# A hybrid encoder layer on one core: the conv branch's token order moves from the rounding and the remainder to the norm's product

## The chip, the cores and the metric

The kernel runs on one core of a Trainium2 chip. The metric is the device time of one execution in microseconds (us); the kernel before takes 1026.38 us, the median of three runs. The core has five engines that each work through a queue of their own in order and wait for one another by semaphores: TensorE (PE, matmuls, results in PSUM banks), VectorE (DVE), ScalarE (ACT), GpSimd (POOL) and SyncE (SP, which here only issues DMAs).

## The reference

One encoder layer over 1024 tokens of 1024 numbers. A convolution branch and an attention branch share the input projection and, side by side, the output projection. The branch that matters here:

```python
def conformer_conv(a, gate, dw_kernel, dw_bias, ln_g, ln_b):
    u = a * jax.nn.sigmoid(gate)
    y = lax.conv_general_dilated(u, dw_kernel[:, None, :], ...)   # depthwise, 31 taps over positions
    y = y + dw_bias
    y = layer_norm(y, ln_g, ln_b)      # over the 512 channels of a token
    return jax.nn.silu(y)
...
        mix = jnp.concatenate([conv_out, attn_out], axis=-1)
        x = x + mix @ w_out[l]
        h = rms_norm(x, norm2_g[l])
        x = x + (jax.nn.silu(h @ w_gate[l]) * (h @ w_up[l])) @ w_down[l]
```

## The kernel before

All matmuls work on numbers split in two: a rounded part in a shorter format (called hi, or the cast) and the remainder (lo). The helper `split` makes both: ACT rounds, and DVE or POOL subtracts the rounded part from the source (lines 108 and 112). The helper `mac` (lines 116 to 118) makes one product of three matmuls: hi by hi, hi by lo of the moving side, lo of the weights by hi.

The token axis is cut in two halves of 512, h = 0 and 1. The attention works on tokens in the order of blocks of the 2-D grid, and its output tiles `at` hold that order: within a half, 4 column blocks b, 16 columns j, 8 rows i. The convolution needs the tokens in their natural order (i, b, j), so its result has to change order before it meets `at` in the output projection. The conv result lies in tiles `u`, one for each of the 4 chunks c of 128 channels; the projection reads its split copies `cm[h]`.

The layer norm of the conv branch goes in steps for each half h: `conv_mean` (PE sums the channels, tile `mr`), `conv_dev` (DVE subtracts the mean at line 894, ACT squares at line 896 into tiles `sd`, POOL adds two of them and DVE the others at lines 898 to 900), `conv_var` (PE transposes into `vs`, DVE sums rows at line 906, ACT takes the root, DVE the reciprocal), `conv_rows` (PE spreads the reciprocals over all partitions, tile `vr` in PSUM, line 918), `conv_norm` for each chunk (DVE multiplies `u` by `vr`, line 921), and `conv_silu` for each chunk (ACT at line 925, then the split into `cm`). In the kernel before, `conv_norm` works in place and in natural order, and the split reads `u` with a step so that `cm` gets the other order.

The output projection `proj` fills banks `pj`, eight blocks m of 128 outputs by two halves: `acc[m, h]`, four k blocks from `at` (k = 4 to 7) and four from `cm` (k = 0 to 3). The kernel runs blocks m = 0 to 3 of half 0 and m = 0, 1 of half 1 over `at` first; each product calls `weave`, which runs the next entry of a list, `woven`. The steps above are placed in it by `slots`, numbered 0 to 19. Then follow the products of `cm` for half 0, k by k, four banks each, with the rest of the `conv_silu` calls woven in. When bank m is complete, `resid` (line 935) adds the input on DVE and frees the bank; block m = 4 needs the bank of m = 0.

The weights of the output projection come in chunks named `wo` + half of the outputs + first k (wo00, wo02, wo04, ...). `take` splits the next one. `WO_SUB` says which engines subtract its halves or quarters: an entry (pool, dve) gives the first half of the columns to POOL and the second to DVE; four times pool makes four pieces on POOL.

The order on every engine is the order in which the code emits instructions; no scheduler changes it.

Of the kernel before, what the change touches and what calls it, by code (L numbers as in the profile page):

```python
# [8 lines left out]
AF = mybir.ActivationFunctionType  # L9
OP = mybir.AluOpType  # L10
# [55 lines left out]
def body(tc, a):  # L66
    from contextlib import ExitStack
    with ExitStack() as ctx:
        build(ctx, tc, a)


def build(ctx, tc, a):
    nc = tc.nc
    pe, act, dve, pool = nc.tensor, nc.scalar, nc.vector, nc.gpsimd
# [5 lines left out]
    def T(tag, shape, bufs, name, dt=F32):  # L80
        return sb.tile(shape, dt, tag=tag, bufs=bufs, name=name)
# [10 lines left out]
    def ST(name, dt=F32):  # L92
        return T("st", [P, 512], 5, name, dt)

    def SM(name, n=8):
        return T("sm", [P, 8], 12, name)[:, :n]
# [4 lines left out]
    def tp(name):  # L101
        return ps.tile([P, 512], F32, tag="tp", bufs=2, name=name)
# [4 lines left out]
    def split(hi, lo, src, sub=(pool,)):  # L107
        act.copy(hi, src)  # L108
        n = src.shape[-1] // len(sub)
        for i, eng in enumerate(sub):  # L110
            sl = slice(i * n, (i + 1) * n)
            eng.tensor_tensor(*[w[..., sl] for w in (lo, src, hi.bitcast(F32))], OP.subtract)  # L112
# [25 lines left out]
    def want(src, name, dst, sub=(pool,)):  # L138
        chunks.append((src, name, dst, sub))
# [72 lines left out]
    def wo_dst(d, k0):  # L212
        def dst():
            if (d, k0 // 4) == (1, 1):
                if not woq:
                    woq.append(H(f"wo{d}{k0}", F32R))
                o = k0 % 4 * 1024
                hl = (woq[0][:, o:o + 1024], woq[0][:, o + 1024:o + 2048])
            else:
                hl = (G(f"wo{d}{k0}h", F32R), G(f"wo{d}{k0}l", F32R))  # L220
            for j in range(2):
                wo[d, k0 + j] = [w[:, j * 512:(j + 1) * 512] for w in hl]
            return hl
        return dst

    WO_SUB = {(0, 2): (pool,) * 4, (1, 0): (dve, pool), (1, 2): (dve, pool), (1, 4): (pool, dve), (1, 6): (pool, dve)}
    for d in range(2):
        for k0 in (4, 6, 0, 2):
            want(a["wo"][k0 * P:(k0 + 2) * P, d * 512:(d + 1) * 512].rearrange("(k p) m -> p k m", p=P),
                 f"wo{d}{k0}", wo_dst(d, k0), WO_SUB.get((d, k0), (pool,)))  # L230

# [34 lines left out]
    eps = T("eps", [P, 1], 1, "eps")  # L266
    dve.memset(eps, EPS)
    warm = SM("warm", 1)
# [410 lines left out]
    def whole(n):  # L679
        return -(-n // 32) * 32  # L680
# [36 lines left out]
    def groups(s_):  # L717
        n, m = width(s_), P if s_ == 0 else 4 * WIN[order[s_][1]][1]
        return [slice(o, min(o + m, n)) for o in range(0, n, m)]
# [66 lines left out]
    def weigh(i):  # L786
        s_, hp = divmod(i, 4)
        rh, cb = order[s_]
        if hp == 0:
            os_[s_] = tp(f"o{s_}").rearrange("p (c q) -> p c q", c=4)  # L790
        gs = groups(s_)
        for g, k in enumerate(gs):
            n = whole(k.stop - k.start)
            v = vwt["first"][:, g, :] if s_ == 0 else vw[cb, rh + g]
            for hh in range(2):
                c = (2 * hp + hh) * HD
                pe.matmul(os_[s_][hh * HD:(hh + 1) * HD, hp], v[:n, c:c + HD], pTs[i][hh][:n, g],  # L797
                          start=g == 0, stop=g == len(gs) - 1)

    def half(name):  # L800
        w = H(name, F32R).rearrange("p (w k s) -> p w k s", w=2, s=512)
        return w[:, 0], w[:, 1]

    def at_of(s_):
        rh, cb = order[s_]
        return [w[:, :, cb * P:cb * P + P] for w in at[rh]]

    def evac_hi(s_):
        if not at:
            at.extend(half(f"at{h}") for h in range(2))  # L810
        act.copy(at_of(s_)[0], os_[s_])

    def evac_lo(s_):
        hi, lo = at_of(s_)
        dve.tensor_tensor(lo, os_[s_], hi.bitcast(F32), OP.subtract)
# [48 lines left out]
    cm, xT, acc = [], {}, {}  # L864
# [15 lines left out]
    cw = {}  # L880

    def of(c, h):
        return u[c][0][:, h * 512:(h + 1) * 512]

    def conv_mean(h):
        cw["m", h] = tp(f"mr{h}")
        for n, w in enumerate(cr[:2]):
            pe.matmul(cw["m", h], cr[2], w[:, h * 512:(h + 1) * 512], start=n == 0, stop=n == 1)

    def conv_dev(h):  # L890
        sq = []
        for c in range(4):
            w = of(c, h)
            dve.scalar_tensor_tensor(w, cw["m", h], -1.0 / 512, w, OP.mult, OP.add)
            sq.append(ST(f"sd{h}{c}"))
            act.activation(sq[c], w, AF.Square)
            if c == 1:
                pool.tensor_tensor(sq[0], sq[0], sq[1], OP.add)
        dve.tensor_tensor(sq[2], sq[2], sq[3], OP.add)
        dve.tensor_tensor(sq[0], sq[0], sq[2], OP.add)  # L900
        cw["s", h] = sq[0]

    def column_rstd(r, pt, w, n):
        for t in range(4):
            pe.transpose(pt[:, t * P:(t + 1) * P], w[:, t * P:(t + 1) * P], ident)
        dve.tensor_reduce(r, pt.rearrange("p (t c) -> p t c", c=P), mybir.AxisListType.X, OP.add)
        act.activation(r, r, AF.Sqrt, bias=eps, scale=1.0 / n)
        dve.reciprocal(r, r)

    def conv_var(h):  # L910
        pt = tp(f"vs{h}")
        cw["v", h] = SM(f"cv{h}", 4)
        column_rstd(cw["v", h], pt, cw["s", h], DC)

    def conv_rows(h):
        cw["r", h] = tp(f"vr{h}")
        for t in range(4):
            pe.transpose(cw["r", h][:, t * P:(t + 1) * P], cw["v", h][:, t:t + 1].to_broadcast([P, P]), ident)

    def conv_norm(h, c):  # L920
        dve.tensor_tensor(of(c, h), of(c, h), cw["r", h], OP.mult)

    def conv_silu(h, c):
        w = of(c, h)
        act.activation(w, w, AF.Silu, bias=lnb[:, c:c + 1], scale=lng[:, c:c + 1])
        hi, lo = [q[:, c].rearrange("p (b j i) -> p b j i", b=4, j=16) for q in cm[h]]
        split(hi, lo, w.rearrange("p (i b j) -> p b j i", b=4, j=16), (dve,))

    def load_xT(m):
        xT[m] = G(f"xT{m}")  # L930
# [14 lines left out]
    for i in range(4, 32, 2):  # L945
# [31 lines left out]
        if jobs:  # L977
# [22 lines left out]
    conv_dev(0)  # L1000

    cm += [half(f"cm{h}") for h in range(2)]
    slots = {0: lambda: (weigh(31), evac_hi(7), evac_lo(7)), 3: lambda: (conv_var(0), conv_mean(1), conv_dev(1)),
             7: lambda: (conv_rows(0), [conv_norm(0, c) for c in range(4)]), 13: lambda: conv_var(1),
             16: lambda: conv_rows(1), 17: lambda: act.activation(warm, eps, AF.Silu),
             19: lambda: (conv_silu(0, 0), conv_norm(1, 0))}
    woven.extend(slots.get(n, lambda: None) for n in range(20))
    ATTN, CONV = (4, 5, 6, 7), (0, 1, 2, 3)
    take()
# [12 lines left out]
    for m in range(4):  # L1022
        load_xT(m)
    later = [(0, c) for c in range(1, 4)] + [(1, c) for c in range(4)]
    woven.extend(lambda q=q: (conv_norm(1, q[1]) if q[0] == 0 else None, conv_silu(*q)) for q in later)
    for k in CONV:
        for m in range(4):
# [491 lines left out]
    def quarter(w, o, t):  # L1519
        return w[:, o + t * 512:o + t * 512 + 512]  # L1520
# [58 lines left out]
    for half in range(2):  # L1579
        acc, part_ = GB[half][:, :256], slice(half * 256, half * 256 + 256)  # L1580
        for k in (QF - 2, QF - 1):
            q = ops[(len(SEQ) - 1) * QF + k]
            mac(acc, [q[:, 2 + h, 3 * P:] for h in range(2)], [q[:, h, part_] for h in range(2)], k == QF - 2, k == QF - 1)
        w = quarter(om["u"], 0, 3)[:, part_]
# [17 lines left out]
```

## Time and profile before

| | |
|---|---|
| Runs | 1026.38 us median of 3 (1026.31 to 1026.93) |
| Profiled execution | 1026.91 us; its span, first to last instruction, 1025.1 us |
| Granted TensorE clock, mean | 0.998 |
| PE, DVE, ACT, POOL busy | 99%, 76%, 47%, 45% of the span |
| Conv norm and output projection, half 0 | about 300 to 338 us of the span |

Times in the views are us from the span's start. A row of a timeline has start, duration, engine, line, operation and tiles (output, then inputs); what stands in brackets is how long the engine was idle before it and what ended that. A busy PE is not a PE at its peak: a matmul of 512 columns is shown as 0.39 us long, and the next one can start 0.23 us after it.

### The profile page before, as it was taken

The page shows a single profiled execution, that of the slowest core. Times are in us where ns is not written, and L with a number is a line of the kernel's source. Part 1 is how long each engine was busy: PE and PEld are TensorE (multiplying, and loading weights), DVE is VectorE, ACT ScalarE, POOL GpSimd, SP SyncE. Part 2 cuts the span into 40 slices and gives each one's busy share as a digit, 9 for nine tenths or more (in the row PEclk, how much of TensorE's full clock was granted, in tenths as well). Part 3 has the DMA queues.
Part 4 walks back from the last instruction along what each step waited for, and adds up shares of the span by engine and source line. Part 5 has one row for each costly group of instructions (what it writes and reads, how often), then busy time and mean ns, then how long its engine had stood idle before and what let it go on. Part 6 is the DMA issues. An engine that isn't in the chain of part 4 may idle for free.

```text
span 1025.1 us, 15102 instructions
## 1 busy us (share of the span) xinstructions
PE 1017.1 (99%) x5258; PEld 849.7 (83%) x5258; DVE 776.8 (76%) x1221; ACT 481.3 (47%) x1043; POOL 466.0 (45%) x389
## 2 busy tenths in 40 slices
PE   9999999999999999999999999999999999999998
PEld 8888888877787888888888888888888888888887
DVE  5788897896767385988787787787777766758875
ACT  7556347837878345523434343343342443433432
POOL 1036675535662456157767567567565200003200
PEclk9999999999999999999999999999999999999999
DMA  9416692236503621134334434444341696633631
GB/s 344 172 49 221 203 236 86 105 110 216 161 22 123 242 88 42 42 113 133 120 118 154 154 104 141 147 136 138 120 152 63 222 373 242 219 103 124 220 118 42
DMA packets 75756, 151.70 MB, mean 148 GB/s; under 512 B 14472, under 2 KB 23560, under 8 KB 75040
## 3 DMA queue, kind: packets, MB, share of 16 engines
q1 hardware_dynamic: 73664, 147.38, 43.1%
q10 hardware_dynamic: 2016, 3.36, 0.9%
q8 instruction: 42, 0.69, 0.3%
q14 instruction: 34, 0.28, 0.1%
HBM read 112.06 MB, written 44.11 MB: 152 GB/s over the span
## 4 chain that ended last, share of the span: by engine, by line
PE 91%; DVE 5%; ACT 2%; issue 1%; POOL 1%; DMA 0%; SPq 0%; DVEq 0%; ACTq 0%; POOLq 0%
PE B L116 6%; PE B L118 6%; PE B L117 6%; PE D L116 4%; PE D L117 4%; PE D L118 4%; PE z L116 3%; PE z L118 3%; PE z L117 3%; PE gl L116 3%; PE gl L117 3%; PE gl L118 3%; DVE cv L377 3%; PE pj L116 2%; PE o L797 2%; PE p L774 2%
## 5 line engine op out<-in xcount | busy, mean ns | idle before, releaser
L377 DVE SCALAR_TENSOR_TENSOR cv<-u,par,cv 128x1009 f32<-128x1009 f32 (+14 forms) x92 | 117.5, 1277 | 2.3
L1545 POOL TENSOR_TENSOR ou<-ou,resm 128x512 f32<-128x512 f32 x8 | 12.7, 1602 | 139.5 <-DVE ou L1536 126.1
L108 ACT CAST op<-sr 128x512 fp32r<-128x512 f32 x77 | 47.6, 619 | 58.3 <-PE B2d L118 26.8
L404 POOL TENSOR_TENSOR pa<-pa,pr 128x1022 f32<-128x1022 f32 (+5 forms) x24 | 58.0, 2417 | 37.1 <-ACT pr L403 33.1
L112 DVE TENSOR_TENSOR op<-sr,op 128x512 fp32r<-128x512 f32 x77 | 58.3, 757 | 18.0 <-ACT op L108 18.0
L108 ACT CAST op<-wd 128x512 fp32r<-128x512 f32 x54 | 33.4, 619 | 29.1 <-DVE wd L1440 18.3
L1092 DVE TENSOR_TENSOR ts<-gu,ts 128x512 f32<-128x512 f32 x38 | 43.9, 1154 | 0.7
L752 ACT ACTIVATE e<-e,mx 128x341 f32<-128x341 f32 (+5 forms) x64 | 35.3, 553 | 18.1 <-DVE mx L747 18.1
L763 POOL TENSOR_SCALAR e<-e,rs 128x341 f32<-128x341 f32 (+5 forms) x64 | 32.9, 527 | 22.1 <-DVE rs L761 21.6
L112 DVE TENSOR_TENSOR op<-wd,op 128x512 fp32r<-128x512 f32 x54 | 37.1, 687 | 1.4 <-ACT op L108 0.4
L747 DVE CUSTOM_DVE_ANT_0 e<-s,tab 128x341 f32<-128x341 f32 (+5 forms) x64 | 27.2, 481 | 13.1 <-PE s L730 10.9
L1353 DVE TENSOR_TENSOR g<-D,g 128x512 f32<-128x512 f32 x22 | 15.2, 690 | 23.1 <-PE D L118 23.1
L431 ACT ACTIVATE sq<-z,r 128x64 f32<-128x64 f32 x96 | 28.3, 330 | 4.8 <-PE z L118 4.8
L1330 ACT ACTIVATE D<-D 128x512 f32<-128x512 f32 x22 | 12.8, 582 | 32.9 <-DVE D L1329 32.9
L403 ACT ACTIVATE pr<-u,par 128x1022 f32<-128x1022 f32 (+5 forms) x24 | 27.0, 1138 | 1.6 <-ACT vs L461 1.6
L935 DVE TENSOR_TENSOR xT<-pj,xT 128x512 f32<-128x512 f32 x16 | 10.8, 684 | 21.2 <-PE pj L118 21.2
L116 PE MATMUL B2d<-op 128*128 128x512 f32 x66 | 25.8, 391 | 0.0
L117 PE MATMUL B2d<-op 128*128 128x512 f32 x66 | 25.7, 389 | 0.0
L118 PE MATMUL B2d<-op 128*128 128x512 f32 x66 | 25.7, 389 | 0.0
L1048 POOL TENSOR_TENSOR sq<-sq,sq 128x512 f32<-128x512 f32 x12 | 16.8, 1401 | 18.6 <-ACT sq L1044 18.4
L774 PEld LDWEIGHTS p<-ident,e 128*128 128x128 f32 (+1 forms) x184 | 19.7, 135 | 6.7 <-POOL e L763 5.1
L774 PE MATMUL p<-ident,e 128*128 128x128 f32 (+1 forms) x184 | 23.9, 277 | 0.0
(1481 smaller groups left out, 3773.9 us busy)
## 6 DMA issues: line engine op xcount, KB each, us to landing
gu<-in_gu SPq DMA_DIRECT2D x44, 512.0 KB
sr<-sd SPq DMA_DIRECT2D x77, 256.0 KB
sd<-sd SPq DMA_DIRECT2D x22, 512.0 KB
wd<-in_wd SPq DMA_DIRECT2D x36, 256.0 KB
sd<-g SPq DMA_DIRECT2D x33, 256.0 KB
x<-in_x SPq DMA_DIRECT2D x8, 512.0 KB
xT<-in_xp SPq DMA_DIRECT2D x8, 512.0 KB
xd<-xT SPq DMA_DIRECT2D x16, 256.0 KB
```

Source lines behind the costliest of these rows:

```text
L108: act.copy(hi, src)
L112: eng.tensor_tensor(*[w[..., sl] for w in (lo, src, hi.bitcast(F32))], OP.subtract)
L116: pe.matmul(acc, lh, rh, start=start, stop=False, skip_group_check=True)
L117: pe.matmul(acc, lh, rl, start=False, stop=False, skip_group_check=True)
L118: pe.matmul(acc, ll, rh, start=False, stop=stop, skip_group_check=True)
L377: dve.scalar_tensor_tensor(acc[:, o], uc[:, i], dwk[:, c, t:t + 1], acc[:, o], OP.mult, OP.add)
L404: pool.tensor_tensor(pa[:, o], pa[:, o], pr[:, o], OP.add)
L431: act.activation(sq[:, h * HD:(h + 1) * HD], z[:, h * HD:(h + 1) * HD], AF.Square, scale=r, accum_out=ss[:, h:h + 1])
L752: act.activation(e, e, AF.Exp, bias=mx.pop((i, hh)), scale=-1.0, accum_out=sums[i][:, hh:hh + 1])
L763: pool.tensor_scalar(es[i][:, hh], es[i][:, hh], rs[:, hh:hh + 1], 1.0, op0=OP.mult, op1=OP.mult)
L774: pe.transpose(pt[:m, g * P:(g + 1) * P], et[i][:, hh, k.start:k.start + m], ident)
L1092: (pool if (i, n) in ON_POOL else dve).tensor_tensor(o, l, r, OP.subtract)
```

## The change

The product of the norm now writes a new tile `cn` (from the ring of five `st` tiles) in the attention's order, reading both `u` and `vr` with a step; silu, rounding and remainder then read and write without steps. Of the steps, the mean and deviations of the second half move one slot on, the row spread of the first half moves from slot 7 to 6 with only one of its four products, the other three come with the table load for silu in slot 19, and the row spread of the second half moves from slot 16 to 18. In `WO_SUB`, the halves of wo10 and wo16 change engines and the remainder of wo12 goes to POOL in four pieces.

```diff
-    WO_SUB = {(0, 2): (pool,) * 4, (1, 0): (dve, pool), (1, 2): (dve, pool), (1, 4): (pool, dve), (1, 6): (pool, dve)}
+    WO_SUB = {(0, 2): (pool,) * 4, (1, 0): (pool, dve), (1, 2): (pool,) * 4, (1, 4): (pool, dve), (1, 6): (dve, pool)}
...
+    cn = {}
+
     def conv_norm(h, c):
-        dve.tensor_tensor(of(c, h), of(c, h), cw["r", h], OP.mult)
+        cn[h, c] = ST(f"cn{h}{c}")
+        o, w, r = cn[h, c], of(c, h), cw["r", h]
+        dve.tensor_tensor(o.rearrange("p (b j i) -> p b j i", b=4, j=16), w.rearrange("p (i b j) -> p b j i", b=4, j=16),
+                          r.rearrange("p (i b j) -> p b j i", b=4, j=16), OP.mult)
 
     def conv_silu(h, c):
-        w = of(c, h)
+        w = cn[h, c]
         act.activation(w, w, AF.Silu, bias=lnb[:, c:c + 1], scale=lng[:, c:c + 1])
-        hi, lo = [q[:, c].rearrange("p (b j i) -> p b j i", b=4, j=16) for q in cm[h]]
-        split(hi, lo, w.rearrange("p (i b j) -> p b j i", b=4, j=16), (dve,))
+        split(cm[h][0][:, c], cm[h][1][:, c], w, (dve,))
...
-    slots = {0: lambda: (weigh(31), evac_hi(7), evac_lo(7)), 3: lambda: (conv_var(0), conv_mean(1), conv_dev(1)),
-             7: lambda: (conv_rows(0), [conv_norm(0, c) for c in range(4)]), 13: lambda: conv_var(1),
-             16: lambda: conv_rows(1), 17: lambda: act.activation(warm, eps, AF.Silu),
-             19: lambda: (conv_silu(0, 0), conv_norm(1, 0))}
+    slots = {0: lambda: (weigh(31), evac_hi(7), evac_lo(7)), 3: lambda: conv_var(0),
+             4: lambda: (conv_mean(1), conv_dev(1)), 6: lambda: (conv_rows(0), conv_norm(0, 0)), 13: lambda: conv_var(1),
+             18: lambda: conv_rows(1),
+             19: lambda: (act.activation(warm, eps, AF.Silu), [conv_norm(0, c) for c in (1, 2, 3)],
+                          conv_silu(0, 0), conv_norm(1, 0))}
```

How the instructions stand on DVE from the reciprocal of the second half's variance to the first residual, in the kernel before (`cm_3273` and `cm_3274` are the halves 0 and 1 of `cm`; `u_538`, `u_954`, `u_1126`, `u_1306` the chunks 0 to 3; `vr_3413` the second half's spread rows; `pj_3163` the bank of m = 0):

```order
L908 RECIPROCAL cv_3396<-cv_3396 128x4
L112 TENSOR_TENSOR cm_3273<-u_538,cm_3273 128x512
L921 TENSOR_TENSOR u_538<-u_538,vr_3413 128x512
L921 TENSOR_TENSOR u_954<-u_954,vr_3413 128x512
L112 TENSOR_TENSOR cm_3273<-u_954,cm_3273 128x512
...
L112 TENSOR_TENSOR cm_3274<-u_1126,cm_3274 128x512
L935 TENSOR_TENSOR xT_3432<-pj_3163,xT_3432 128x512
```

The same place in the changed kernel (`cn_3368`, `cn_3426`, `cn_3428`, `cn_3430` are the products of half 0, `cn_3435`, `cn_3451`, `cn_3462` those of half 1; `vr_3363` the first half's rows, `vr_3417` the second half's):

```order
L908 RECIPROCAL cv_3394<-cv_3394 128x4
L925 TENSOR_TENSOR cn_3426<-u_954,vr_3363 128x512
L925 TENSOR_TENSOR cn_3428<-u_1126,vr_3363 128x512
L925 TENSOR_TENSOR cn_3430<-u_1306,vr_3363 128x512
L112 TENSOR_TENSOR cm_3273<-cn_3368,cm_3273 128x512
L925 TENSOR_TENSOR cn_3435<-u_538,vr_3417 128x512
L925 TENSOR_TENSOR cn_3451<-u_954,vr_3417 128x512
L112 TENSOR_TENSOR cm_3273<-cn_3426,cm_3273 128x512
...
L112 TENSOR_TENSOR cm_3274<-cn_3462,cm_3274 128x512
L939 TENSOR_TENSOR xT_3437<-pj_3163,xT_3437 128x512
```

Three products of the first half now stand between the reciprocal and the first remainder; before, they stood ahead of the row sum. What stands ahead of the first residual is otherwise the same.

On POOL, from the wo00 remainder to the first sum of the next norm, as a difference (`sd` are the squares of the second half):

```order
 L112 TENSOR_TENSOR wo00l<-wo00r,wo00h 128x1024
-L898 TENSOR_TENSOR sd_3326<-sd_3326,sd_3329 128x512
 L112 TENSOR_TENSOR wo02l<-wo02r,wo02h 128x256 x4
-L112 TENSOR_TENSOR wo_3479<-wo14r,wo_3479 128x512
-L112 TENSOR_TENSOR wo_3479<-wo16r,wo_3479 128x512
+L898 TENSOR_TENSOR sd_3343<-sd_3343,sd_3346 128x512
+L112 TENSOR_TENSOR wo_3487<-wo14r,wo_3487 128x512
+L112 TENSOR_TENSOR wo_3487<-wo16r,wo_3487 128x512
 L112 TENSOR_TENSOR wo10l<-wo10r,wo10h 128x512
-L112 TENSOR_TENSOR wo12l<-wo12r,wo12h 128x512
```

The sum of two squares of the second half now stands behind the four pieces of wo02 instead of ahead of them, and the wo02 cast on ACT has moved in the same way ahead of the squares.

## The prediction

> **What bounds the kernel now.** I read the page first, then who waited for whom on PE, then PE's timeline where it waits, and last the engines it waits for. The page says that TensorE is the bound:
>
> ```profile
> PE 1017.1 (99%) x5258; PEld 849.7 (83%) x5258; DVE 776.8 (76%) x1221; ACT 481.3 (47%) x1043; POOL 466.0 (45%) x389
> ```
>
> The change adds no matmul and takes none away, so it can only move the time in which PE stands or is clocked down. PE's waits between 300 and 345 us, the stretch of the conv branch's norm (line, who it waited for, us in total, times, longest):
>
> ```profile
> PE pj L116 <- DVE xT L935: 1.9, 1, 1.9
> PE pj L117 <- DVE cm L112: 0.6, 1, 0.6
> ```
>
> PE's timeline at both places (start us, us, line, output<-inputs):
>
> ```profile
> 318.83 0.39 PE L118 MATMUL pj<-at,wo06l 128*128 128x512 f32 x1
> 319.21 0.50 PE L116 MATMUL pj<-cm,wo00h 128*128 128x512 f32 x1
> 320.30 0.50 PE L117 MATMUL pj<-cm,wo00h 128*128 128x512 f32 x1 [0.59 <-DVE cm L112]
> ...
> 330.63 0.39 PE L117 MATMUL pj<-cm,wo02h 128*128 128x512 f32 x1
> 330.86 0.39 PE L118 MATMUL pj<-cm,wo02l 128*128 128x512 f32 x1
> 333.18 0.47 PE L116 MATMUL pj<-at,wo 128*128 128x512 f32 x1 [1.93 <-DVE xT L935]
> ...
> 337.60 0.39 PE L116 MATMUL pj<-cm,wo10h 128*128 128x512 f32 x1
> ```
>
> Undisturbed, a matmul starts 0.23 us after the one before (330.63, 330.86). *Stall one*: the second conv matmul was due at 318.83 + 2 x 0.23 = 319.29 and started at 320.30, so 1.01 us are lost: 0.15 for the rounded block, the rest for its remainder. *Stall two*: the next was due at 331.09 and started at 333.18: 2.09 us. *Slow clock*: from 333.18 to 337.60 stand 12 matmuls in 4.42 us, where 12 x 0.227 = 2.72 would do: 1.70 us. The windows view shows why (us, then busy us of each engine, then the granted clock):
>
> ```profile
> 317.20:320.60 3.40, 2.81 (x11) 1.80 (x10) 1.41 (x2) 3.34 (x5) 0.00 (x0) 1.00 0.96 352
> 330.80:334.20 3.40, 1.47 (x6) 0.90 (x6) 2.81 (x3) 3.37 (x5) 1.28 (x1) 0.98 0.09 34
> 334.20:337.60 3.40, 3.40 (x9) 2.62 (x8) 3.39 (x5) 3.01 (x4) 2.40 (x2) 0.52 0.95 298
> ```
>
> A stretch with PE busy for 1.47 of 3.40 us is followed by one at a clock of 0.52; after stall one (2.81 busy) the clock stayed at 1.00. [...] Together the three losses are 1.01 + 2.09 + 1.70 = 4.80 us.
>
> Both stalls end on DVE, which stands behind ACT's chain of silu and cast:
>
> ```profile
> 315.82 0.18 DVE L908 RECIPROCAL cv<-cv 128x4 f32<-128x4 f32 x1 [0.36 <-ACT cv L907]
> 319.19 1.06 DVE L112 TENSOR_TENSOR cm<-u,cm 128x512 fp32r<-128x512 f32 x1 [3.19 <-ACT cm L108]
> 331.38 1.06 DVE L112 TENSOR_TENSOR cm<-u,cm 128x512 fp32r<-128x512 f32 x1 [0.76 <-ACT cm L108]
> 332.35 0.68 DVE L935 TENSOR_TENSOR xT<-pj,xT 128x512 f32<-128x512 f32 x1
> 317.21 0.80 ACT L925 ACTIVATE u<-u,par 128x512 f32<-128x512 f32 x1
> 318.04 1.11 ACT L108 CAST cm<-u 128x512 fp32r<-128x512 f32 x1
> 319.06 0.81 ACT L925 ACTIVATE u<-u,par 128x512 f32<-128x512 f32 x1
> 330.24 1.11 ACT L108 CAST cm<-u 128x512 fp32r<-128x512 f32 x1
> ```
>
> The residual (L935) that frees PE's bank could not start before 332.35, because the remainder of chunk 2 of the second half stands ahead of it on DVE and waited for its cast, which ended at 331.35. A chunk costs ACT 319.06 - 317.21 = 1.85 us.
>
> **The change part by part.** The prices (by shape: count, busy us, mean ns):
>
> ```profile
> L108 ACT CAST cm<-u 128x512 fp32r<-128x512 f32 x8 | 9.0, 1124 | 0.3
> L108 ACT CAST crh<-cs 128x512 fp32r<-128x512 f32 x2 | 1.2, 617 | 0.0
> L108 ACT CAST wo<-wo14r 128x1024 fp32r<-128x1024 f32 x1 | 1.1, 1051 | 0.0
> L112 DVE TENSOR_TENSOR cm<-u,cm 128x512 fp32r<-128x512 f32 x8 | 8.7, 1088 | 6.0 <-ACT cm L108 6.0
> L921 DVE TENSOR_TENSOR u<-u,vr 128x512 f32<-128x512 f32 x8 | 5.1, 678 | 0.0
> L112 DVE TENSOR_TENSOR wo<-wo14r,wo 128x512 fp32r<-128x512 f32 x1 | 0.7, 686 | 0.0
> L898 POOL TENSOR_TENSOR sd<-sd,sd 128x512 f32<-128x512 f32 x2 | 2.6, 1292 | 3.8 <-ACT sd L896 3.8
> L112 POOL TENSOR_TENSOR wo10l<-wo10r,wo10h 128x512 fp32r<-128x512 f32 x1 | 1.8, 1839 | 1.6 <-ACT wo10h L108 1.6
> ```
>
> *Casts.* Eight stop reading with a step: 1.12 becomes 0.62, 0.50 us each. A chunk then costs ACT 1.85 - 0.50 = 1.35 us.
> *Remainders.* Eight fall from 1.09 to 0.69.
> *Products.* Eight of 0.68 now read u and vr with a step, vr from PSUM. No row has that. Below, a gain is excluded: the cast and the remainder both got dearer by the same step. The nearest row is the remainder with one stepped input, 1.09 (0.41 more than the dense product); if the two steps add, 0.68 + 2 x 0.41 = 1.50, and PSUM could be dearer yet. I take 1.09, since both inputs walk the same steps side by side. Products follow each other by some 0.08 less than they take, so 1.0.
>
> *Steps placed anew.* The wo02 cast now stands ahead of the second half's squares on ACT, and its four POOL pieces ahead of POOL's sum of two squares. With these rows
>
> ```profile
> 307.27 0.30 ACT L907 ACTIVATE cv<-cv,eps 128x4 f32<-128x4 f32 x1 [1.97 <-DVE cv L906]
> 311.90 3.25 POOL L112 TENSOR_TENSOR wo02l<-wo02r,wo02h 128x256 fp32r<-128x256 f32 x4 [0.78 <-ACT wo02h L108]
> 311.77 0.69 DVE L900 TENSOR_TENSOR sd<-sd,sd 128x512 f32<-128x512 f32 x1
> 314.04 0.60 PE L905 MATMUL vs<-ident,sd 128*128 128x128 f32 x4
> 314.77 0.69 DVE L906 TENSOR_REDUCE cv<-vs 128x4 f32<-128x512 f32 x1
> ```
>
> the walk is: the root ends at 307.57; the cast, 1.05, at 308.6; the pieces, 3.25, at 311.9; POOL's sum, 1.29, at 313.2; DVE's last sum, 0.69, at 313.9 (before: 312.46). Behind PE's wait for it would stand everything, but PE comes to the transposes only at 314.04: the cover is 0.1 us. If DVE and POOL get in each other's way there (POOL's wo10 half took 1.84 beside DVE, 1.29 is its usual price), it is 0.55 late: 0.45 of PE, and stall one below grows by 0.1. That stays within the forecast.
>
> Then DVE's queue: first product 313.9 to 315.0; the row sum starts at 315.0 instead of 314.77. So root, table load and first silu come about 0.25 later: silu at 317.45, cast from 318.3 to 318.9. PE comes at 319.06, so the 0.15 goes. DVE's reciprocal ends at 316.25, and three products now stand ahead of the first remainder: 3 x 1.0, to 319.25. The remainder, 0.69, ends at 319.95, and PE's second conv matmul starts at 320.0: stall one is 0.7, not 1.01. **Saved: 0.3.**
>
> What is late next: products 10 and 11 end at 321.85, the remainder of chunk 1 at 322.55; PE wants it 12 matmuls on, at 320.0 + 12 x 0.227 = 322.7. It holds by 0.15, and the later ones by over 1 us, since only one product then stands ahead of each.
>
> Stall two: ACT starts chunk n at 317.45 + 1.35 n, and behind the fifth chunk comes the wo14 cast (0.95 until the next may start). Chunk 6 (the second half's third) starts at 317.45 + 8.1 + 0.95 = 326.5 and its cast ends at 327.95; DVE's remainder is done by 328.7. PE's last matmul for that bank is followed by nine for the three others, so it starts 10 x 0.227 ahead of 331.09, at 328.82, and ends 0.39 later, at 329.2; less 0.3 that is 328.9. The residual runs to 329.65, and PE wants the bank at 330.8. Stall two is covered by 1.15 us: **2.09 saved**, and with it the **1.70** of slow clock.
>
> *Weight remainders.* wo16's halves change engines; its cast ends at 328.9, each half takes 0.69 to 1.84, PE wants the pieces from 332.1 on. wo10's first half goes to POOL: cast done at 331.3, half at 332.6 to 333.15, wanted at 333.9. wo12 goes to POOL in four pieces of 0.81 behind it, the first done by 334.0, the third by 335.6, wanted at 335.3 and 336.0. None reaches PE; if POOL were slower still by 0.55 per piece, about 1 us would. On SP, the loads behind the wo12 load (it waits for the wo02 pieces) go out 3 us earlier; the xT4 to xT7 loads follow the first residual, as PE does.
>
> **Sum**: 0.3 + 2.09 + 1.70 = 4.1 us. The profiled execution took 1026.91 (span 1025.1 and 1.8 around it): 1022.8. The median of the runs is 0.53 below that execution, so I forecast 1022.3.
>
> **The rivals.** A measurement of this kernel can tell 0.2%, 2.05 us, from no change. All but the last two hang on the price d of the stepped product: each 0.1 us more makes stall one 0.4 longer (four products stand ahead of the first remainder), and past d = 1.17 the next wait 0.2 longer (six products stand ahead of the second remainder).
>
> *Steps add, d = 1.50* (0.14): stalls of 0.7 + 1.6 and 0.65, 2.95 in all. If the clock holds, 4.80 - 2.95 = 1.85 are saved (1024.5); if it falls for 1.70 us, 0.15 (1026.2). For it: no row shows the product. Half of it counts as faster: a little less price or split windows, half as same.
>
> *Slower: DVE becomes the bound at the first remainder* (0.09). From d = 1.5 on, stalls and a clock fall eat the whole gain; from d = 1.86 the kernel is over 2.05 us slower: 0.55 + 0.6 x 7.7 = 5.2, and 1.70, against 4.80. At d = 2.0 it is 0.55 + 5.5 + 1.70 - 4.80 = 2.95 slower, 1029.3. Against it: one step costs 0.41, not 1.3. [...]
>
> *The clock falls anyway* (0.07): what set it to 0.52 at 334.2 was not the stall, and comes again. Then only 0.3 + 2.09 = 2.4 are saved, 1024.0. Against it: 0.52 stands right behind the stall, and the other windows shown have 0.98 and 1.00. [...]
>
> *The gain is given back later* (0.08): the next stage's transfers, busy at 0.95 in the window from 334.2, become what PE waits for, and 2 to 4 us return: 1024.4 to 1026.4. Against it: no wait of PE there names a DMA, and the loads move forward with the residual.
>
> **How the numbers follow.** The forecast has 0.62. Faster: 0.62 + 0.07 + half of 0.14 = 0.76; same: 0.07 + 0.08 = 0.15; slower: 0.09. Low end: all 4.80 and 0.2 for spread, 1021.4. High end 1025.5: it takes in the clock rival, most of the adding steps and some of the giving back, and leaves out under 0.2.
>
> **What would show it.** Right: products near 1.09, casts near 0.62, remainders near 0.69; a first stall near 0.7; no wait of L116 for the first residual; a clock of 1.00 from 330 to 340. Wrong: a product over 1.5, a low clock after 320, or PE waiting at the transposes of 314.

## The result and the profile after

The changed kernel takes 1022.0 us, the median of six runs (1021.64 to 1022.5). The kernel before took 1026.45 us in the six runs beside them (1025.2 to 1026.93). The ratio is 0.9958, with a 95% interval of 0.9945 to 0.9971: faster by 0.42%, twice the 0.2% that the prediction takes as the least that can be told from no change. The forecast was 1022.3 us. The profiled execution went from 1026.91 to 1022.48 us and its span from 1025.1 to 1020.6, 4.5 us less.

From the page after, the engines' busy time. With the same 5258 matmuls PE is shown busy for 2.9 us less; 1.70 us of that are the twelve matmuls that ran at the slow clock before and were shown longer, the rest was not followed up:

```profile
PE 1014.2 (99%) x5258; PEld 847.3 (83%) x5258; DVE 777.3 (76%) x1220; ACT 477.2 (47%) x1043; POOL 466.9 (46%) x392
```

PE's waits between 300 and 345 us, after. The residual's wait of 1.9 us has no row any more, and the remainder's fell from 0.6 to 0.2:

```profile
PE pj L117 <- DVE cm L112: 0.2, 1, 0.2
```

PE's timeline at the two places, after:

```profile
318.94 0.40 PE L118 MATMUL pj<-at,wo06l 128*128 128x512 f32 x1
319.18 0.39 PE L116 MATMUL pj<-cm,wo00h 128*128 128x512 f32 x1
319.73 0.50 PE L117 MATMUL pj<-cm,wo00h 128*128 128x512 f32 x1 [0.16 <-DVE cm L112]
...
330.29 0.39 PE L118 MATMUL pj<-cm,wo02l 128*128 128x512 f32 x1
330.52 0.39 PE L116 MATMUL pj<-at,wo 128*128 128x512 f32 x1
...
333.24 0.39 PE L116 MATMUL pj<-cm,wo10h 128*128 128x512 f32 x1
...
335.96 0.39 PE L116 MATMUL pj<-at,wo 128*128 128x512 f32 x1
```

Stall one: the second conv matmul was due at 318.94 + 2 x 0.23 = 319.40 and started at 319.73, 0.33 us late instead of 1.01. Stall two: block m = 4 starts 0.23 us after the matmul ahead of it (330.29, 330.52), so nothing is left of 2.09. From there to wo10 it takes 333.24 - 330.52 = 2.72 us for 12 matmuls, where it was 4.42: nothing is left of the 1.70 either. Together 0.68 + 2.09 + 1.70 = 4.47, the 4.5 us by which the span fell. The windows of the second stall's place, after (the third number from the right is the granted clock; it was 0.98 and 0.52):

```profile
330.80:334.20 3.40, 3.40 (x17) 2.81 (x16) 3.40 (x5) 2.22 (x4) 2.87 (x3) 1.00 0.96 305
334.20:337.60 3.40, 3.40 (x17) 2.82 (x16) 1.57 (x3) 2.18 (x4) 3.32 (x5) 1.00 1.03 320
```

The prices, after, by shape (count, busy us, mean ns of one):

```profile
L925 DVE TENSOR_TENSOR cn<-u,vr 128x512 f32<-128x512 f32 x8 | 8.4, 1085 | 0.1
L112 DVE TENSOR_TENSOR cm<-cn,cm 128x512 fp32r<-128x512 f32 x8 | 6.4, 821 | 0.0
L108 ACT CAST cm<-cn 128x512 fp32r<-128x512 f32 x8 | 5.0, 622 | 0.3
```

The product rose from 0.68 to 1.09 us, the cast fell from 1.12 to 0.62. The remainders' mean of 0.82 is that of seven at about 0.69 and one at 1.7, which ran while POOL did its half of wo14.

### The profile page after: what moved, and what is told of

Same layout as the page of the kernel before. It is cut to its first block, busy times and chain, and to the rows that moved or that the text cites. A ratio compares the mean times of both kernels' runs of the same rounds, so it can differ in the third digit from the quotient of the medians.

```text
span 1020.6 us, 15104 instructions
## 1 busy us (share of the span) xinstructions
PE 1014.2 (99%) x5258; PEld 847.3 (83%) x5258; DVE 777.3 (76%) x1220; ACT 477.2 (47%) x1043; POOL 466.9 (46%) x392
## 4 chain that ended last, share of the span: by engine, by line
PE 96%; DVE 2%; DMA 1%; POOL 1%; issue 1%; ACT 1%; SPq 0%; DVEq 0%; ACTq 0%; POOLq 0%
PE B L116 6%; PE B L117 6%; PE B L118 6%; PE z L116 4%; PE z L118 4%; PE z L117 4%; PE D L116 4%; PE D L117 4%; PE D L118 4%; PE gl L118 3%; PE gl L117 3%; PE gl L116 3%; PE pj L116 2%; PE pj L117 2%; PE pj L118 2%; PE p L774 2%
```

## The experiments

Executions reach the stage at times that differ by up to 1.0 us. So the traces are compared by one number, the *distance*: from the first matmul of the norm's mean (L888, second half, near 300 us) to the start of block m = 5, which is the 335.96 above. Both stalls, the slow clock and what may follow at wo10 and wo12 lie between them. The clock fell in the traced executions of the kernel before and of the places alone, but not in every execution of these kernels, as is told below; so for these two the medians and the distances tell slightly different things.

| Kernel | L888 | m = 5 | Distance | Median, us (runs) |
|---|---|---|---|---|
| before | 299.97 | 340.34 | 40.37 | 1026.45 (6) |
| after | 300.09 | 335.96 | 35.87 | 1022.0 (6) |
| product alone | 300.07 | 337.55 | 37.48 | 1023.52 (7) |
| places alone | 299.09 | 339.31 | 40.22 | 1025.68 (11) |
| after, old table of remainders | 299.96 | 335.92 | 35.96 | 1022.08 (5) |
| before, 9 matmuls in the stall | 299.37 | 339.24 | 39.87 | 1026.0 (11) |
| before, 4 matmuls in the stall | 299.21 | 339.10 | 39.89 | 1025.94 (11) |
| after, product and copy apart | 299.48 | 337.17 | 37.69 | 1023.6 (11) |
| after, step on the write | 299.14 | 335.01 | 35.87 | 1021.47 (1) |
| after, other order on VectorE | 299.36 | 335.06 | 35.70 | 1021.47 (5) |
| after, other order, once more | 300.04 | 335.80 | 35.76 | 1021.52 (5) |
| after, once more | 299.86 | 335.73 | 35.87 | 1022.29 (5) |

### The product alone, the places alone

The first kernel has the new product, silu and split with the old `slots` and the old table; the second has the old product with the new `slots` and table. In short, against the changed kernel:

```diff
 # product alone
-    WO_SUB = (new); slots = (new)
+    WO_SUB = (old); slots = (old)
 # places alone
-    conv_norm, conv_silu = (new)
+    conv_norm, conv_silu = (old)
```

> The new product, silu and split, with the old slots and the old halves of the weights. Theory (the cheaper casts on ACT's chain make the gain): the four first-half products, 1.0 each instead of 0.6, stand ahead of the row sum, which comes some 1.5 us later; stall one about 1.2 to 1.5 instead of 0.32, no stall two, clock 1.00: 1022.9 to 1023.2. Rival (the new places make the gain): stall two stays and the time stays near 1026.4.

> The old product and split with the new slots and the new halves of the weights. Theory: casts still 1.12, stall two near 2.1 and the clock fall stay, 1026.0 to 1027.0. Rival (the places make the gain): stall two gone, near 1022.

Measured: the product alone 1023.52 us, 0.9973 (0.9962 to 0.9983) of the kernel before; the places alone 1025.68, 0.9991 (0.9982 to 1.0). By distance, the product alone saves 2.89 us, the places alone 0.15, both together 4.50: 1.46 us come only when both are there. Neither time lies in its expected range: the first came 0.3 us above 1022.9 to 1023.2, the second 0.3 below 1026.0 to 1027.0. What the product does without the places is seen in PE's longer wait of that kernel:

```profile
PE vr L918 <- DVE cv L908: 1.0, 1, 1.0
```

and in its DVE timeline:

```profile
312.48 4.08 DVE L925 TENSOR_TENSOR cn<-u,vr 128x512 f32<-128x512 f32 x4
316.47 0.69 DVE L906 TENSOR_REDUCE cv<-vs 128x4 f32<-128x512 f32 x1
317.52 0.18 DVE L908 RECIPROCAL cv<-cv 128x4 f32<-128x4 f32 x1 [0.36 <-ACT cv L907]
```

All four products of the first half, now 4.08 us long, stand ahead of the row sum, so the reciprocal comes at 317.52 instead of 315.82, and PE, which comes to the spread of the rows in slot 16, waits 1.04 us for it. This wait was not foreseen; stall one behind it is 0.52 us, not the 1.2 to 1.5 expected. The new places take the wait away: one product ahead of the row sum, and the spread two slots later. The second stall and the slow clock do not come in this kernel (no wait for `xT` in its rows, a clock of 1.00 from 330.8 to 337.6). Without the product, the places leave the second stall as it was; PE's timeline of that kernel:

```profile
329.87 0.39 PE L118 MATMUL pj<-cm,wo02l 128*128 128x512 f32 x1
332.18 0.64 PE L116 MATMUL pj<-at,wo 128*128 128x512 f32 x1 [1.92 <-DVE xT L935]
```

The median of the places alone is 0.66 us below the 1026.34 of the kernel before in the same measurement, the distance only 0.15. Part of the rest lies behind m = 5: from there to the end of the span this kernel takes 684.39 us, the kernel before 684.76, and PE's wait of 0.5 us for a reciprocal of the next norm, near 358 us, is there in the kernel before and not in this one.

### The table of weight remainders alone

```diff
-    WO_SUB = {(0, 2): (pool,) * 4, (1, 0): (pool, dve), (1, 2): (pool,) * 4, (1, 4): (pool, dve), (1, 6): (dve, pool)}
+    WO_SUB = {(0, 2): (pool,) * 4, (1, 0): (dve, pool), (1, 2): (dve, pool), (1, 4): (pool, dve), (1, 6): (pool, dve)}
```

> The changed kernel with the old table of the weight remainders (second rows of wo10 and wo12 half on DVE, half on POOL, as before). Theory, the stepped product and the places of the steps carry the gain and the table only follows: the block of output chunk 5 starts on TensorE 35.9 us after the first norm matmul, as in the changed kernel (35.87), no wait of TensorE from the table, 1022.0 us (1021.7 to 1022.4). Rival, without the new table the remainders of wo10 and wo12 come late, as they did in the kernel with nine matmuls more in the stall (waits of 0.41 us at wo10's remainder, a block 1.0 us longer): the block of chunk 5 starts 36.3 to 37.0 us after the first norm matmul, 1022.4 to 1023.2 us.

Measured: 1022.08 us, 0.9959 (0.9947 to 0.9972); distance 35.96 against 35.87; PE's only wait is the 0.2 us of stall one. The table is worth about 0.1 us at most. So all but that of the 1.46 us belongs to the slots.

### Is the clock's fall a loss of its own?

The kernel before, with nine, and with four, matmuls into an unused bank just where PE stands in stall two. Nothing waits for them.

```diff
+    idle = tp("idle")
+    for _ in range(9):     # 4 in the second kernel
+        pe.matmul(idle, wo[0, 4][0][:, :P], at[0][0][:, 0], start=True, stop=True)
     for m in range(4, 8):
         load_xT(m)
```

> The kernel before, with nine extra matmuls into an unused bank between the last conv product of half 0 and block m = 4: 9 x 0.227 = 2.04 us of PE work inside the stall of 2.09. Theory (PE's idle time sets the clock down): the first real matmul still starts near 333.2, but the clock stays at 1.00 and 1.70 us are saved, 1024.7. Rival (the clock falls anyway): 0.52 again behind it, 1026.4.

> As the kernel with nine, with four extra matmuls (0.9 us): PE is busy for about 2.4 of the 3.4 us where before 1.47 and where 2.81 did not lower the clock. If a share near half decides, the clock stays at 1.00 and the time is 1024.7; if any gap of a microsecond is enough, it falls and the time is 1026.4.

Measured: 1026.0 us, 0.9998 (0.9989 to 1.0007), and 1025.94, 0.9996 (0.9987 to 1.0004). The kernel before beside them has 1026.34, so no gain can be told, and the 1024.7 expected of a clock that stays up did not come. Windows of the kernel with nine, then the first of these of the one with four:

```profile
330.80:334.20 3.40, 3.40 (x16) 2.54 (x15) 3.39 (x4) 3.37 (x4) 1.29 (x1) 1.00 0.26 90
334.20:337.60 3.40, 3.00 (x14) 2.13 (x13) 3.40 (x4) 2.27 (x4) 2.98 (x2) 1.00 0.97 331
```

```profile
330.80:334.20 3.40, 2.33 (x11) 1.63 (x10) 3.39 (x4) 3.37 (x4) 1.27 (x1) 1.00 0.31 95
```

and PE's row in which the stall of the one with four ends:

```profile
332.48 0.47 PE L116 MATMUL pj<-at,wo 128*128 128x512 f32 x1 [1.07 <-DVE xT L935]
```

The clock stays at 1.00 in both. One trace of each would not settle it, since the clock does not fall in every execution of the kernel before: a fall to one half for 3.4 us of 1025 lowers the mean granted clock by 0.0017, and in this measurement 19 of its 29 executions have a mean of 0.998 and 10 of 1.000. Of the kernels with extra matmuls, all 22 executions have 1.000. So it was PE's standing still that brought the fall, and the rival by which the clock falls anyway is refuted.

But the 1.70 us did not come back as time. The kernel before shows the same: its executions with 0.998 have a median of 1026.45 us, those with 1.000 of 1025.97, which is the time of the kernels with extra matmuls. Here the fall costs 0.5 us; in the two other measurements of the kernel before it costs 1.5 (7 executions of 15) and 1.2 (6 of 9). No execution without the fall was traced, so it is not shown that its stall was as long. PE's timeline with nine matmuls shows where the 1.70 us went:

```profile
330.49 2.20 PE L1035 MATMUL idle<-at,wo04h 128*128 128x512 f32 x9
...
335.50 0.39 PE L116 MATMUL pj<-cm,wo10h 128*128 128x512 f32 x1
335.72 0.39 PE L117 MATMUL pj<-cm,wo10h 128*128 128x512 f32 x1
336.52 0.50 PE L118 MATMUL pj<-cm,wo10l 128*128 128x512 f32 x1 [0.41 <-DVE wo10l L112]
...
338.21 0.50 PE L118 MATMUL pj<-cm,wo12l 128*128 128x512 f32 x1
...
339.24 0.40 PE L116 MATMUL pj<-at,wo 128*128 128x512 f32 x1
```

From L888 to wo10 this kernel is 1.50 us quicker than the kernel before (335.50 - 299.37 = 36.13; 337.60 - 299.97 = 37.63). Then the wo10 block waits for its remainder, 0.57 us in all, and wo12's block 0.18, and the stretch from wo10 to m = 5 takes 3.74 us instead of 2.74. Of 1.50 us, 1.0 is given back. DVE's half of the wo10 remainder, with nine matmuls and then in the kernel before:

```profile
334.66 1.80 DVE L112 TENSOR_TENSOR wo10l<-wo10r,wo10h 128x512 fp32r<-128x512 f32 x1
```

```profile
335.21 0.68 DVE L112 TENSOR_TENSOR wo10l<-wo10r,wo10h 128x512 fp32r<-128x512 f32 x1
```

Two things make it late. Behind the long casts it starts only at 334.66, and beside POOL, which subtracts the other half from 334.62 on, it takes 1.80 us instead of 0.68; at 0.68 it would have ended at 335.34, ahead of the 335.95 at which PE wants it. In the kernel before it is POOL's half that is long (1.84), and PE, at the slow clock, comes to these remainders only from 338.06 on. Why now the one engine and now the other pays is not known. In the changed kernel DVE's half, now the second, takes 1.79 as well, but with ACT's shorter chain it starts at 331.50 and ends at 333.29, and PE wants it at 334.37. In the changed kernel with the old table, where DVE's half is the first again, PE takes it at 333.56 and shows no wait for it. So the same change that removes the stall also brings these remainders in time.

### Why not a dense product and a copy?

```diff
-        dve.tensor_tensor(o.rearrange(...), w.rearrange(...), r.rearrange(...), OP.mult)
+        dve.tensor_tensor(w, w, r, OP.mult)
+        dve.tensor_copy(o.rearrange("p (b j i) -> p b j i", b=4, j=16), w.rearrange("p (i b j) -> p b j i", b=4, j=16))
```

> The changed kernel with the product made of two operations, the dense product (0.68) and a copy that reads with a step (about 1.09): the price d of the prediction's slower rival set to about 1.6 per product from start to start instead of 1.0. Theory (products ahead of the first remainder make stall one, 0.4 per 0.1 of price): stall one 0.32 + 2.4 = 2.7, the next wait 1.0 to 1.3, the clock falls once for 1.7, no stall two: 5.4 to 5.7 lost against 4.80 before, 1027.0 to 1027.5. If the clock holds, 1025.5. Rival (DVE has room, ACT's chain is what counts): near 1022.3.

Measured: 1023.6 us, 0.9978 (0.9969 to 0.9987). None of the expected times (1027.0 to 1027.5, 1025.5 and 1022.3) came. The expectation priced the copy like the remainder with a step, 1.09. Its groups on DVE:

```profile
L925 DVE TENSOR_TENSOR u<-u,vr 128x512 f32<-128x512 f32 x8 | 5.4, 677 | 0.0
L926 DVE COPY cn<-u 128x512 f32<-128x512 f32 x8 | 5.4, 675 | 0.3
```

The copy took 0.60 to 0.64 us, but for one of 1.01 beside POOL, and the next instruction starts 0.55 us after it. A product and a copy take 1.25 us of DVE, a stepped product 1.0. Four of them stand ahead of the first remainder, so it should come 4 x 0.25 = 1.0 us later. PE's timeline:

```profile
318.34 0.40 PE L118 MATMUL pj<-at,wo06l 128*128 128x512 f32 x1
...
320.18 0.50 PE L117 MATMUL pj<-cm,wo00h 128*128 128x512 f32 x1 [1.16 <-DVE cm L112]
```

Stall one is 320.18 - 318.80 = 1.38 us, 1.05 more than in the changed kernel. That is the sensitivity the prediction used (0.4 us of stall for each 0.1 us of price), seen at work. The rest of the 1.82 us by which the distance grew is lost later: 0.29 up to the next conv remainder, 0.37 from there to m = 4, 0.10 behind it. The window around it has PE busy for 2.24 of 3.40 us at a clock of 1.00, and no later window up to 341 us has less:

```profile
317.20:320.60 3.40, 2.24 (x12) 1.51 (x11) 3.33 (x6) 3.31 (x6) 0.00 (x0) 1.00 0.68 272
```

### Which step costs what

Three kernels ask for the price of the step. In the first the product reads densely and writes with a step. In the second the four chunks use four forms; in the third four others. The code is written shorter here: `o4` is `cn` in the attention's order, `ws[0]` and `rs[0]` are `u` and `vr` read with the step, `ws[1]` and `rs[1]` read densely. The second and third multiply or copy numbers of the wrong tokens in some chunks, so only their prices are read (one execution each, 1022.02 and 1022.45 us).

```diff
 # step on the write
+        dve.tensor_tensor(o.rearrange("p (b j i) -> p i b j", b=4, j=16), w.rearrange("p (i b j) -> p i b j", b=4, j=16),
+                          r.rearrange("p (i b j) -> p i b j", b=4, j=16), OP.mult)
 # one input: c = 0 both stepped, 1 only u, 2 only vr, 3 neither
+        dve.tensor_tensor(o4, ws[c > 1], rs[c % 2], OP.mult)
 # forms: c = 0 vr first and stepped, u dense; 1 vr first and dense, u stepped; 2 and 3 dense product, then a copy
+        dve.tensor_copy(o4, ws[1])    # c = 2: dense
+        dve.tensor_copy(o4, ws[0])    # c = 3: stepped
```

> The changed kernel with the same product, but both inputs read densely and the step in the write of cn. If the step costs the same on the writing side, the product takes 1.09 again and nothing else changes (1022.0). If writes with a step are free, it takes 0.68, stall one (0.32) is gone and the time is 1021.7.

> The changed kernel with four forms of the product: chunk 0 reads both inputs with the step, chunk 1 only u (SBUF), chunk 2 only vr (PSUM), chunk 3 neither; chunks 1 to 3 multiply numbers of different tokens, so the output is not the layer's. If the two steps run side by side and cost the same: 1.09, 1.09, 1.09, 0.68. If PSUM's step is free: chunk 2 at 0.68. If PSUM's step is the dearer one and hides SBUF's: chunk 1 below chunks 0 and 2.

> The changed kernel with four other forms of the norm's product; chunks 0 to 2 of the layer get tokens in a wrong order. Chunk 0: first input the PSUM tile, stepped, second the SBUF tile, dense. Chunk 1: first input PSUM, dense, second SBUF, stepped. Chunk 2: dense product, then a dense copy. Chunk 3: dense product, then a copy with stepped reads. Theory one, the step costs where SBUF is read: chunk 0 at 0.68 us, chunk 1 at 1.07. Theory two, it costs on the first input alone: chunk 0 at 1.07, chunk 1 at 0.68. For the copies: if a step costs a one-input instruction nothing, dense and stepped both 0.55 to 0.68 us (stepped took 0.60 to 0.64); if a dense copy is faster and the step takes that away, dense 0.30 to 0.45. Time between 1022 and 1023.5 us; only the prices are read.

Measured, by groups on DVE. The step on the write:

```profile
L925 DVE TENSOR_TENSOR cn<-u,vr 128x512 f32<-128x512 f32 x8 | 8.8, 1170 | 0.1
```

One input (L929 both stepped, L931 only `u`, L933 only `vr`, L935 neither):

```profile
L929 DVE TENSOR_TENSOR cn<-u,vr 128x512 f32<-128x512 f32 x2 | 2.1, 1075 | 0.0
L931 DVE TENSOR_TENSOR cn<-u,vr 128x512 f32<-128x512 f32 x2 | 2.1, 1072 | 0.0
L935 DVE TENSOR_TENSOR cn<-u,vr 128x512 f32<-128x512 f32 x2 | 1.4, 684 | 0.0
L933 DVE TENSOR_TENSOR cn<-u,vr 128x512 f32<-128x512 f32 x2 | 1.4, 683 | 0.0
```

Other forms (L929 and L931 have `vr` as the first input; L934 and L937 are the copies):

```profile
L931 DVE TENSOR_TENSOR cn<-vr,u 128x512 f32<-128x512 f32 x2 | 2.1, 1064 | 0.0
L929 DVE TENSOR_TENSOR cn<-vr,u 128x512 f32<-128x512 f32 x2 | 1.4, 680 | 0.0
L937 DVE COPY cn<-u 128x512 f32<-128x512 f32 x2 | 1.3, 637 | 0.1
L934 DVE COPY cn<-u 128x512 f32<-128x512 f32 x2 | 0.9, 426 | 0.1
```

The step costs 0.39 us where `u` is read from SBUF (1.07 against 0.68), as first input or as second. Where `vr` is read from PSUM it costs nothing, first or second (0.68 with the step in both places, 0.68 without). So the two steps do not add (1.07 with both, 1.07 with that of `u` alone), because one of them is free. The copy pays 0.21 us for its step (0.64 against 0.43): cheap, not free. The product with the step on the write is shown longer (1.17 in the mean), but costs DVE's queue the same: in both kernels the three products and the start of the remainder behind them lie 2.94 us apart, and the distance is 35.87 in both. None of the stepped products is far from 1.09, so the rivals from 1.50 and 1.86 on have no ground.

### Another order on VectorE

Two products instead of three stand ahead of the first remainder, and the second half's products stand behind the remainders of the first half:

```diff
-             19: lambda: (act.activation(warm, eps, AF.Silu), [conv_norm(0, c) for c in (1, 2, 3)],
-                          conv_silu(0, 0), conv_norm(1, 0))}
+             19: lambda: (act.activation(warm, eps, AF.Silu), [conv_norm(0, c) for c in (1, 2)],
+                          conv_silu(0, 0), conv_norm(0, 3))}
...
-    woven.extend(lambda q=q: (conv_norm(1, q[1]) if q[0] == 0 else None, conv_silu(*q)) for q in later)
+    woven.extend(lambda n=n, q=q: (conv_silu(*q), conv_norm(1, n) if n < 4 else None) for n, q in enumerate(later))
```

> The changed kernel with another order on DVE: two first-half products instead of three stand ahead of the first remainder, and each second-half product stands behind the remainder of a first-half chunk. Theory (DVE's queue ahead of the first remainder makes the rest of stall one): the remainder starts with its cast's end, near 318.85 instead of 318.99, stall one falls from 0.32 to 0.15 to 0.2 and no other wait comes: 1021.8, which a measurement can't tell from the changed kernel's 1022.0; the trace can.

> The changed kernel with VectorE's other order (a first remainder ahead of the fourth product), once more beside the changed kernel. If the rest of stall one (0.32 us) is all that it removes: 0.15 to 0.35 us less than the changed kernel beside it, 1021.6 to 1021.9 us. If what it saves there is given back later: within 0.1 us of it.

> The changed kernel once more, on the chip of the other three: 1022.0 us (1021.6 to 1022.4), block of chunk 5 35.9 us after the first norm matmul. It is what the kernels with the old table and with the other order are held against.

Measured: 1021.47 us, 0.9958 (0.9945 to 0.9972), and on another chip 1021.52, 0.9952 (0.9939 to 0.9966), beside the changed kernel at 1022.29, 0.9959 (0.9947 to 0.9972). PE's timeline of the second of them:

```profile
318.88 0.40 PE L118 MATMUL pj<-at,wo06l 128*128 128x512 f32 x1
...
319.53 0.50 PE L117 MATMUL pj<-cm,wo00h 128*128 128x512 f32 x1
```

Stall one is down from 0.33 to 319.53 - 319.34 = 0.19 us. DVE stood idle 0.73 us ahead of that remainder, waiting for the cast, so now the cast sets it, and moving more products behind it can't take more. The distance fell by 0.11 to 0.17 us. The medians differ by 0.77 us, more than that and more than the 0.15 to 0.35 expected, but the runs overlap (1021.14 to 1022.03 against 1021.63 to 1022.5), and the intervals do too. Part of it lies later: in both traces of the changed kernel PE waits 0.49 us for a reciprocal of the next norm, near 358 us, and in both traces of this order it does not. It does not in the kernel with the old table either, whose DVE order at the stall is the changed kernel's. What decides that wait was not found.

## Why the prediction was right

The mechanism came as forecast: both stalls fell on the steps named, and the slow clock went with the second. The forecast was 0.3 us too high, nearly all of it from one mis-sized term, stall one. By its own steps:

- **Product, 1.09 taken between bounds of 1.09 and 1.50.** Measured 1.085. The choice of the low bound was right, its reason (both inputs walk the same steps side by side) was not: the PSUM input's step is free, and stepping `u` alone costs the same 1.07. That the low bound held was luck. The prediction also weighed that PSUM could be dearer yet; here DVE read `vr` with the step in 0.68 us, as densely (0.68).
- **Stall one, forecast 0.7, measured 0.33.** This is the term that was mis-sized, by nearly 0.4. DVE's timeline after shows it:

```profile
313.32 0.69 DVE L900 TENSOR_TENSOR sd<-sd,sd 128x512 f32<-128x512 f32 x1 [1.18 <-POOL sd L898]
313.93 1.07 DVE L925 TENSOR_TENSOR cn<-u,vr 128x512 f32<-128x512 f32 x1
314.92 0.68 DVE L906 TENSOR_REDUCE cv<-vs 128x4 f32<-128x512 f32 x1
315.96 0.18 DVE L908 RECIPROCAL cv<-cv 128x4 f32<-128x4 f32 x1 [0.36 <-ACT cv L907]
316.05 3.03 DVE L925 TENSOR_TENSOR cn<-u,vr 128x512 f32<-128x512 f32 x3
318.99 0.69 DVE L112 TENSOR_TENSOR cm<-cn,cm 128x512 fp32r<-128x512 f32 x1
```

  The walk let only the products overlap. In fact the others here also start before the one ahead of them is shown to end, by 0.08 to 0.09 us: the product after the sum (313.93 against 314.01), the row sum after the product (314.92 against 315.00), the products after the reciprocal (316.05 against 316.14), the remainder after them (318.99 against 319.08). Those four make 0.34 of it. This execution came to the stage 0.12 us later, DVE and PE alike, which does not change the stall.
- **The cover of 0.1 us at 314.** The wo02 pieces took 2.84 instead of 3.25, and POOL's sum 1.75 instead of 1.29, beside a sum on DVE of 1.12. The two errors cancel by luck (last sum at 313.32, forecast from 313.2), and PE did not wait at the transposes. The contention that the prediction priced at 0.55 did come, at 0.46.
- **Stall two.** Silu of the seventh chunk was forecast at 326.5 and came at 326.52; the residual ran from 329.19 to 329.87, forecast to 329.65. PE took the bank at 330.52: the slack was 0.65, not 1.15, still cover. The 2.09 us were saved whole.
- **Slow clock.** Between the two traces the 1.70 us were saved whole, and the cause was the stall, as the kernels with extra matmuls show (a mean clock of 1.000 in all 22 executions). But the prediction took the fall from one traced execution as part of the kernel; it came in 32 of the 53 further executions. In the measurement of "after, once more" (1022.29) the kernel before has 1026.88 with the fall and 1025.71 without, so 4.59 or 3.42 us are saved. And the prediction counted the fall as a loss that ends with the stall. It does so only if the remainders of wo10 and wo12 are in time as well; in the kernel before they would have eaten 1.0 us of it. Here they are, since ACT rounds wo10 at 330.21 instead of 334.07. The prediction named this cover as "none reaches PE" for the changed kernel and was right; the rival by which the gain is given back later was the real danger, though through late remainders, not through transfers.
- **Weight remainders.** The table is worth at most 0.1 us, as walked.

## What to carry to other kernels

Put a change of order on the instruction whose engine waits ahead of the chain, not on the engine that paces the chain: eight casts 0.50 us shorter on ACT were worth eight products 0.41 us longer on DVE. They were worth 2.89 us as they stood, and 4.50 once most of the products had been moved from in front of the row sum that others wait for. Before a stall and a slow clock are added up as a gain, fill the stall with idle matmuls: what then waits next is the part of the sum that will not come unless the change speeds that up too. In a walk along one engine's queue, take the distance between starts as the price, not the duration shown (here 1.0 us for a product shown as 1.09).

## What the runs showed of the hardware

**The clock fell to one half behind a stall of 2.09 us, in some executions only, and in one trace about 0.9 us after the stall's end.** In half-microsecond windows of the kernel before (the stall lies from 331.09 to 333.18):

```profile
333.50:334.00 0.50, 0.50 (x4) 0.41 (x3) 0.50 (x1) 0.50 (x1) 0.14 (x1) 1.00 0.22 82
334.00:334.50 0.50, 0.50 (x3) 0.39 (x2) 0.48 (x2) 0.50 (x2) 0.00 (x0) 0.58 1.05 385
...
337.00:337.50 0.50, 0.50 (x3) 0.40 (x2) 0.50 (x1) 0.21 (x1) 0.50 (x2) 0.51 1.02 418
337.50:338.00 0.50, 0.50 (x3) 0.42 (x3) 0.50 (x2) 0.00 (x0) 0.50 (x1) 1.00 1.17 369
```

and of the kernel with the places alone (stall from 330.10 to 332.18):

```profile
332.50:333.00 0.50, 0.50 (x2) 0.35 (x2) 0.50 (x1) 0.50 (x1) 0.14 (x1) 0.50 0.23 86
...
335.50:336.00 0.50, 0.50 (x3) 0.36 (x3) 0.50 (x2) 0.50 (x2) 0.50 (x2) 0.77 0.94 369
```

A stall of 2.09 us brought a clock of 0.50 for about 3.4 us (estimated from the windows: about 334.1 to 337.5 in the kernel before), in the one kernel about 0.9 us after PE had resumed, in the other (stall of 2.08) within 0.32 us of it. It did not do so every time: by the mean clock in 32 of 53 executions of the kernel before and in 6 of 11 of the places alone. A stall of which four matmuls left 1.23 us (332.48 - 331.25) brought no fall in any of 11 executions, and one of 1.38 us none in its trace. No run shows what sets the length of the fall, its changing distance from the stall, or why it comes in some executions only.

**The price of a step of 256 bytes on DVE**, for 128x512 float32 values: 0.39 us where a two-input instruction reads SBUF (1.07 against 0.68), whether that input alone is stepped or the PSUM input too; as much by the distance of starts where it writes SBUF (2.94 us for three products with the step on the read and with it on the write); 0.21 in a copy (0.64 against 0.43); nothing where it reads PSUM (0.68 against 0.68).
